# A hybrid decoder step in split fp32: grouping an item's products by the part of its weight tile

## The chip, the cores and the metric

One core of a Trainium2 chip (trn2) runs the whole step as one program. The metric is the device time of one execution in microseconds (us). The profile is one further execution, recorded by the hardware profiler.

## The reference

One layer of a hybrid decoder, for 512 prompt tokens and 8 x 4 sample tokens, all in fp32, with D = 2048:

```
h   = rms_norm(x, norm_mix_w)
b_a, c_a, h_a, q, k, v, z, a, b = split(h @ w_in)            # 7 x 1024 + 16 columns
y_a = rms_norm(b_a * dwconv3(c_a * h_a))                     # 8 channel groups
o   = rms_norm(gated_delta(silu(dwconv4(q, k, v)), a, b)) * silu(z)   # 8 heads of 128
x  += concat(y_a, o) @ w_out                                 # 2048 x 2048
h   = rms_norm(x, norm_ffn_w)
x  += square(relu(h @ w_up)) @ w_down                        # 2048 x 8192 and back
return rms_norm(x, final_norm_w), new conv states, new delta states
```

Nearly all of the arithmetic is in the four matrix products (w_in, w_out, w_up, w_down). The delta rule is a chain of small triangular systems and state updates for each head.

## The kernel before

**Split products.** TensorE multiplies fp32r values, which hold fewer bits than fp32. So each operand is split into a rounded part (hi) and the remainder (lo = value - hi), and a product is the sum of three matmuls: w_hi with x_hi, w_hi with x_lo, w_lo with x_hi. All three add up in one PSUM tile. A matmul takes a 128x128 block of a weight and 272 columns (256 prompt and 16 sample tokens) of the activations; the two halves of the tokens are h = 0 and 1.

**The stream of weights.** Weights come in items of up to 128x1024, eight blocks. `weight` (L110) loads an item by SyncE's DMA queue into a raw tile (w_raw, 2 buffers), ScalarE converts it to w_hi (L118), VectorE subtracts to w_lo (L121); both have 3 buffers. `ahead` (L46) asks for an item two items before it is multiplied. In the order of instructions, an item of eight blocks and one half is 24 matmuls, one with both halves 48.

**Where the products are issued.** `product` (L139) issues the three matmuls of one block (six with both halves), then the next block follows. It is called in the first stage (L248: three slabs of w_in against k tiles as x arrives; each item has blocks of two k tiles), in the rest of w_in (L855), in the output projection in two parts (w_o1, L906, and w_o2, L942), in the plain up blocks (L975), in w_d0 (L1178) and in the last part of w_down (L1266). From there on, up and down are done by a bilinear scheme (`bilinear`, L1064) with seven products in place of eight for a 2x2 block of weights and activations, in the order 1, 2, 5, 6, 7, 3, 4; it has a copy of the three-matmul loop (L1088). Its weights are sums of four quarters (w_q): VectorE forms w_s (L1052) and the other sums (L1054 to L1056) from loaded quarters, then ScalarE converts (L1060) and VectorE subtracts (L1061). The results are copied to u by ScalarE (L1121) or added (L1127 up, L897 down) by VectorE.

**Side work.** During w_in, the delta rule of four groups of heads runs between the projection's matmuls. `run_side` (L802) lets a generator issue its next part after every 12 matmuls of the projection. One group's chain is: an elimination loop on VectorE (L556, L560), a way through DRAM into tn and tt, a transpose of tn (L574), triangular products on TensorE (L594, L606, L611, L617, L623) with copies by VectorE between them, then four steps along the sequence (L637 to L663: st times k, r times tt, y times ke). The sum of squares of x (ssq, L246) feeds the first norm (`rstd_rows`, L152).

**What sets the order.** A scheduler of the tile framework orders each engine's instructions by priorities and by its own model of when operands are ready; `urgent` raises the priority of loads, conversions and of what frees PSUM. So the order on ScalarE, VectorE and SyncE's queue follows also from the order in which the code issues the products.

Of the kernel before, what the change touches and what calls it, by code (L numbers as in the profile page):

```python
# [18 lines left out]
P = 128  # L19
D = 2048  # L20
KT = D // P
# [11 lines left out]
N_START = 3  # L33
# [3 lines left out]
N1 = 8  # L37
# [18 lines left out]
def trunk(ctx, tc, a):  # L56
    nc = tc.nc
    V, S, G, PE = nc.vector, nc.scalar, nc.gpsimd, nc.tensor
# [77 lines left out]
            V.scalar_tensor_tensor(lo, src, w, hi.bitcast(F32), MUL, SUB)  # L136
        return hi, lo

    def product(ps, w, c, x, start, stop, halves=(0, 1)):  # L139

        (whi, wlo), (xhi, xlo) = w, x
        for i, (wp, xp) in enumerate(((whi, xhi), (whi, xlo), (wlo, xhi))):
            for h in halves:
                x = xp[h] if isinstance(xp, tuple) else xp[:, h, :]
                PE.matmul(ps[h], wp[:, c : c + P], x, start=start and i == 0, stop=stop and i == 2)  # L145

    def rstd_rows(out, ssqs, t, halves=(0, 1)):

# [29 lines left out]
    with ExitStack() as mix:  # L178
# [39 lines left out]
        for kp in range(KT // 2):  # L218
            with urgent():
                xr = tile_in(dp, "xr", [P, 2, 2, HT], tag=("gt", "qd", "vs")[kp % 3])  # L220

            def first():
                h_x.append(split(xr[:, 0], 0))

            with urgent():
                if kp:
                    nc.sync.dma_start(xr, a["x"][kp])
                else:
                    nc.sync.dma_start(nv, a["nv"])
                    tc.keep_in_program_order(nc.sync.dma_start(xr[:, 0], a["x"][kp][:, 0]))  # L230
            w = weight(a["w_first"][kp], 2 * N_START * P, None if kp else first)
            if kp == 0:
                with urgent():
                    tc.keep_in_program_order(nc.sync.dma_start(xr[:, 1], a["x"][kp][:, 1]))
            for j in range(2):
                k = 2 * kp + j
                with urgent():
                    if k:
                        h_x.append(split(xr[:, j], k))
                    sq = tmp2()  # L240
                    square = S.activation(sq, xr[:, j], AF.Square)
                    if k == 0:
                        tc.keep_in_program_order(square)
                        V.tensor_copy(ssq, sq)
                    else:
                        (G if k < KT - 2 else V).tensor_tensor(ssq, ssq, sq, ADD)  # L246
                for s in range(N_START):
                    product(first_ps[s][0], w, (j * N_START + s) * P, h_x[k], k == 0, k == KT - 1)  # L248
            if kp == 3:
                with urgent():  # L250
                    nc.sync.dma_start(wab, a["w_ab"])
# [597 lines left out]
        for (s, hf), w in ahead(srcs, lambda it: weight(a["w_in"][2 * it[0] + it[1]], 1024)):  # L849
            if hf == 0:  # L850
                job = next(jobs)
                ps = ps_big()
            for k in range(8):
                kk = 8 * hf + k
                product(ps[0], w, k * P, h_x[kk], kk == 0, kk == KT - 1)  # L855
                if k % 2:
                    run_side()
            if hf == 1:
                job(ps)
        assert next(jobs, None) is None  # L860
# [39 lines left out]
    for (ob, q), w in ahead([(o, q) for o in range(KT) for q in range(2)],  # L900
                            lambda it: weight(a["w_o1"][2 * it[0] + it[1]], N1 // 2 * P)):
        if q == 0:
            ps = ([ps_small(HT) for _ in range(2)], None) if ob in (2, 3) else ps_big()
        for k in range(N1 // 2):
            kk = N1 // 2 * q + k
            product(ps[0], w, k * P, cat[kk], kk == 0, kk == N1 - 1)  # L906
        if q == 1 and ps[1] is not None:
            add(x2[ob], ps[1])
        elif q == 1:
            for h in range(2):  # L910
                add(x2[ob][:, h], ps[0][h])
# [26 lines left out]
    steps = [(h, o) for h in range(2) for o in range(KT)]  # L938
    for (h, ob), w in ahead(steps, lambda it: weight(a["w_o2"][it[1]], N2 * P)):
        ps = ps_small(HT)  # L940
        for k in range(N2):
            product({h: ps}, w, k * P, cat[N1 + k], k == 0, k == N2 - 1, (h,))  # L942
        add(x2[ob][:, h], ps)
        sq = tile_in(sqp, "sq", [P, HT])
        S.activation(sq, x2[ob][:, h], AF.Square)
        if ob == 0:
            G.tensor_copy(ssq[:, h, :], sq)
        else:
            (G if ob < KT - 2 else V).tensor_tensor(ssq[:, h, :], ssq[:, h, :], sq, ADD)
        if ob % 2:  # L950
            nc.gpsimd.dma_start(x2_d[ob // 2][:, :, h, :], x2p[ob // 2][:, :, h, :])
        if h == 1:
            if ob == 1:
                rstd_rows(r2, [ssq], t_tile("rt", "T")[:, 0:2], (0,))
            if ob >= 2 and ob % 2 == 0 or ob == KT - 1:
                i = ob // 2 - 1 if ob < KT - 1 else KT // 2 - 1
                normalise(i, 0)
                hi, lo = c_tile(hlp, "c0_hi"), c_tile(hlp, "c0_lo")
                parts_into(hi, lo, x2p[i][:, :, 0, :])
                h_c[i].update({1: (hi[:, 0], lo[:, 0]), 2: (hi[:, 1], lo[:, 1])})  # L960
# [4 lines left out]
    def plain(m, h):  # L965
        t = t_tile("u", "u")
        u = t[:, :2]
        for i in range(2):
            ps = ps_small(HT)
            for j in range(2):  # L970
                with urgent():
                    w = weight(a["w_up"][m, 2 * i + j], 1024)
                for k in range(KT // 2):
                    x = h_c[k][1 + j] if h == 0 else (d_c[k][0][:, j], d_c[k][1][:, j])
                    product({h: ps}, w, k * P, tuple((t, t) for t in x), j == k == 0, j == 1 and k == 7, (h,))  # L975
            with urgent():
                S.activation(u[:, i], ps, AF.Relu)
        with urgent():
# [85 lines left out]
    def bilinear(items, early, cs, outs):  # L1064
# [13 lines left out]
        for (w, p), (whi, wlo) in ahead(items, load):  # L1078
# [3 lines left out]
                w.ps["y" if p == 2 else "z"] = bank(False)  # L1082
            ps = w.ps[{2: "y", 5: "z", 3: "z"}.get(p, "x")]
            c = cs(w.key)
            for k, ck in enumerate(c):
                xhi, xlo = ck[p]
                for j, (wp, xp) in enumerate(((whi, xhi), (whi, xlo), (wlo, xhi))):
                    PE.matmul(  # L1088
                        ps, wp[:, k * P : (k + 1) * P], xp,
                        start=p in (1, 2, 5) and k == j == 0, stop=k == len(c) - 1 and j == 2,  # L1090
                        skip_group_check=True,
                    )
            w.out(p, ps)

    T_AT = {1: 0, 3: 1, 2: 2, 6: 3, 5: 4, 7: 5, 4: 6}
# [77 lines left out]
    for q, w in ahead(range(KT // 4), lambda q: weight(a["w_d0"][q], 1024)):  # L1173
        for j in range(4):
            ob = 4 * q + j
            ps = [bank(True), bank(False)]
            for k in range(2):
                product(ps, w, (2 * j + k) * P, u_0[k], k == 0, k == 1)  # L1178
            for h in range(2):
                add(x2[ob][:, h], ps[h])  # L1180
    late.close()
# [78 lines left out]
    for (h, q), ws in ahead(steps, lambda it: last_weight(it[1]), 1):  # L1260
        for j in range(2):
            ob = 2 * q + j
            x = x2[ob][:, h]
            ps = ps_small(HT)
            for k in range(4):
                product({h: ps}, ws[j], k * P, u[k], k == 0, k == 3, (h,))  # L1266
            add(x, ps)
            sq = tile_in(cmb2, "sq", [P, 2, HT], tag="c")
            with urgent():
# [148 lines left out]
```

## Time and profile before

| | us |
|---|---|
| median of 3 runs (lowest, highest) | 2495.59 (2492.95, 2500.96) |
| the profiled execution | 2508.89 |
| span of its trace | 2507.1 |
| TensorE busy in it | 2435.8 |
| VectorE, ScalarE, GpSimdE busy | 1821.1, 1105.4, 498.3 |
| mean granted TensorE clock | 0.979 |

The stages in the trace, by the time at which their matmuls run: first stage 0 to 53, w_in with the delta groups 53 to 860, w_o1 860 to 955, w_o2 955 to 1052, plain up 1052 to 1133, bilinear up 1133 to 1762, w_d0 1762 to 1796, bilinear down 1796 to 2434, the last part of down 2437 to 2492, the final norm to the end. In the trace's rows an engine's idle time stands in brackets with what ended it. "PEld" is TensorE's weight load, which overlaps matmuls. A matmul's recorded duration (290 ns) is longer than the distance from one start to the next (about 125 ns), since matmuls are pipelined.

### The profile page before, as it was taken

To read this page: it belongs to the slowest core of one execution; us is meant where nothing else is said; L and a number is where in the kernel's file an instruction comes from. 1 tells how busy PE (TensorE), PEld (TensorE's weight loads), DVE (VectorE), ACT (ScalarE), POOL (GpSimd) and SP (SyncE) were. 2 spreads that over 40 slices of the span, in tenths; PEclk is the share of its full clock that TensorE was granted. 3 is DMA by queue.
4 is the path that set the end of the run, shared out by engine and by line. 5 is a ranking of instruction groups with operands and counts; after the bars stand their busy time and mean duration, and the time that the engine had idled before them with its cause. 6 is when DMAs were issued, how large, how long until landed. Compare 5 with 4: busy or idle time off the path is not lost.

```text
span 2507.1 us, 47369 instructions
## 1 busy us (share of the span) xinstructions
PE 2435.8 (97%) x19065; PEld 2389.9 (95%) x19065; DVE 1821.1 (73%) x2993; ACT 1105.4 (44%) x1628; POOL 498.3 (20%) x783
## 2 busy tenths in 40 slices
PE   8999999999999999999999999999899999999997
PEld 8999999999999899989999999999799999999996
DVE  8676575567557635788888888888488787878795
ACT  5425333332532524565555555555233333333346
POOL 4124113212312303310111111111401111111003
PEclk9999998999998999999999999999899999999998
DMA  6233333332423536565565555556846666566323
GB/s 197 91 106 110 94 101 98 112 97 88 135 88 92 200 106 205 187 195 200 193 228 195 195 194 189 188 190 220 320 127 195 195 195 193 191 194 193 108 84 106
DMA packets 145812, 400.76 MB, mean 160 GB/s; under 512 B 35540, under 2 KB 46456, under 8 KB 145592
## 3 DMA queue, kind: packets, MB, share of 16 engines
q1 hardware_dynamic: 109368, 265.56, 33.7%
q0 software_dynamic: 36224, 132.16, 14.6%
q8 instruction: 150, 2.46, 0.4%
q14 instruction: 70, 0.57, 0.1%
HBM read 318.76 MB, written 78.89 MB: 159 GB/s over the span
## 4 chain that ended last, share of the span: by engine, by line
PE 56%; issue 23%; DVE 9%; DMA 6%; POOL 3%; ACT 2%; SPq 0%; POOLq 0%; DVEq 0%; ACTq 0%
PE ps_big L145 25%; PE ps_s L1088 23%; PE ps_sm L145 3%; DVE w_lo L121 3%; DMA w_raw<-in_w_o_dram 2%; DMA w_raw<-in_w_up_dram 1%; POOL ucd L1106 1%; POOL ucd L1105 1%; DMA w_q<-in_w_d_dram 1%; ACT w_hi L118 1%; DVE xm L560 1%; PE ps_s L145 1%; DVE tm L556 1%; DMA tn<-ti 1%; DVE x2v L897 1%
## 5 line engine op out<-in xcount | busy, mean ns | idle before, releaser
L1088 PE MATMUL ps_s<-uc,w_hi 128*128 128x272 f32 x3248 | 621.1, 291 | 10.8 <-ACT w_hi L1060 8.3
L1060 ACT ACTIVATE w_hi<-w_q 128x768 fp32r<-128x768 f32 (+6 forms) x440 | 382.6, 873 | 544.7 <-PE ps_s L1088 395.3
L1088 PEld LDWEIGHTS ps_s<-uc,w_hi 128*128 128x128 f32 x3248 | 510.8, 189 | 20.4 <-ACT w_hi L1060 11.4
L1061 DVE TENSOR_TENSOR w_lo<-w_q,w_hi 128x768 fp32r<-128x768 f32 (+6 forms) x440 | 434.2, 989 | 61.0 <-ACT w_hi L1060 58.3
L1088 PE MATMUL ps_s<-uc,w_lo 128*128 128x272 f32 x1624 | 462.9, 289 | 0.3
L145 PE MATMUL ps_big<-x_hi,w_hi 128*128 128x272 f32 x1984 | 425.1, 294 | 0.9 <-ACT x_hi L133 0.7
L145 PE MATMUL ps_big<-x_hi,w_lo 128*128 128x272 f32 x1984 | 420.8, 292 | 2.4 <-DVE w_lo L121 2.4
L145 PE MATMUL ps_big<-x_lo,w_hi 128*128 128x272 f32 x1984 | 420.5, 293 | 0.3 <-DVE x_lo L136 0.3
L118 ACT ACTIVATE w_hi<-w_raw 128x1024 fp32r<-128x1024 f32 (+3 forms) x211 | 206.9, 980 | 402.9 <-PE ps_big L145 249.5
L121 DVE TENSOR_TENSOR w_lo<-w_raw,w_hi 128x1024 fp32r<-128x1024 f32 (+3 forms) x211 | 269.8, 1279 | 138.5 <-ACT w_hi L118 135.8
L145 PEld LDWEIGHTS ps_big<-x_hi,w_hi 128*128 128x128 f32 x1984 | 317.2, 190 | 5.0 <-issue 1.4
L145 PEld LDWEIGHTS ps_big<-x_hi,w_lo 128*128 128x128 f32 x1984 | 316.3, 191 | 3.9 <-DVE w_lo L121 3.0
L145 PEld LDWEIGHTS ps_big<-x_lo,w_hi 128*128 128x128 f32 x1984 | 315.9, 191 | 0.9 <-DVE x_lo L136 0.5
L1088 PEld LDWEIGHTS ps_s<-uc,w_lo 128*128 128x128 f32 x1624 | 304.6, 189 | 2.3 <-DVE w_lo L1061 1.9
L1088 PE MATMUL ps_s<-c_hi,w_lo 128*128 128x272 f32 x928 | 267.7, 289 | 2.2 <-DVE w_lo L1061 1.5
L1088 PE MATMUL ps_s<-c_hi,w_hi 128*128 128x272 f32 x928 | 266.6, 287 | 0.5 <-ACT w_hi L118 0.5
L1088 PE MATMUL ps_s<-c_lo,w_hi 128*128 128x272 f32 x928 | 266.3, 287 | 0.0
L1159 POOL DMA_DIRECT2D uc<-ucd x203 | 110.4, 548 | 439.5 <-PE ps_s L1088 411.0
L897 DVE TENSOR_TENSOR x2v<-x2v,ps_s 128x272 f32<-128x272 f32 x347 | 148.6, 434 | 67.5 <-PE ps_s L1088 59.1
L1088 PEld LDWEIGHTS ps_s<-c_hi,w_lo 128*128 128x128 f32 x928 | 174.4, 188 | 3.2 <-DVE w_lo L1061 2.1
L1088 PEld LDWEIGHTS ps_s<-c_hi,w_hi 128*128 128x128 f32 x928 | 174.5, 188 | 0.7 <-ACT w_hi L118 0.7
L1088 PEld LDWEIGHTS ps_s<-c_lo,w_hi 128*128 128x128 f32 x928 | 174.5, 188 | 0.0
(378 smaller groups left out, 4270.7 us busy)
## 6 DMA issues: line engine op xcount, KB each, us to landing
w_q<-in_w_up_dram SPq DMA_DIRECT2D x116, 512.0 KB, 4.3
uc<-ucd POOLq DMA_DIRECT2D x203, 272.0 KB, 5.3
w_raw<-in_w_in_dram SPq DMA_DIRECT2D x106, 512.0 KB, 3.4
w_q<-in_w_d_dram SPq DMA_DIRECT2D x128, 384.0 KB, 3.7
w_raw<-in_w_o_dram SPq DMA_DIRECT2D x32, 512.0 KB, 3.4
ucd<-u_hi POOLq DMA_DIRECT2D x29, 544.0 KB, 5.4
ucd<-tc POOLq DMA_DIRECT2D x29, 544.0 KB, 6.7
w_raw<-in_w_up_dram SPq DMA_DIRECT2D x28, 512.0 KB, 3.6
```

The costliest lines, as they stand in the source:

```text
L118: S.activation(hi[:, c], raw[:, c], AF.Copy)
L121: V.tensor_tensor(lo[:, c], raw[:, c], hi[:, c].bitcast(F32), SUB)
L145: PE.matmul(ps[h], wp[:, c : c + P], x, start=start and i == 0, stop=stop and i == 2)
L556: V.tensor_tensor(t, xm[:, :, j : j + 1].broadcast_to([P, 8, n]), um[:, j : j + 1, j + 1 :].broadcast_to([P, 8, n]), MUL,)
L560: V.tensor_tensor(xm[:, :, j + 1 :], xm[:, :, j + 1 :], t, SUB)
L897: V.tensor_tensor(out, out, ps, ADD)
L1060: S.activation(hi, s, AF.Copy)
L1061: V.tensor_tensor(lo, s, hi.bitcast(F32), SUB)
L1088: PE.matmul(ps, wp[:, k * P : (k + 1) * P], xp, start=p in (1, 2, 5) and k == j == 0, stop=k == len(c) - 1 and j == 2, skip_group_check=True,)
L1105: nc.gpsimd.dma_start(d[:, at : at + n], hi.bitcast(F32))
L1106: nc.gpsimd.dma_start(d[:, 7 + at : 7 + at + n], src)
L1159: nc.gpsimd.dma_start(t.bitcast(F32), uc_d[KS[j]][:, 2 * b : 2 * b + 2])
```

## The change

Within an item, the matmuls are ordered by the part of the weight. For all its blocks come w_hi with x_hi and w_hi with x_lo, block by block, and then for all its blocks w_lo with x_hi. In the first stage, whose items hold blocks of two k tiles, the passes are w_hi with x_hi, w_lo with x_hi, w_hi with x_lo, each over all blocks of the item. `products` is a generator that yields after every six (block, pass) pairs where side work runs between them, which is again every 12 matmuls. The matmuls are the same, as are the numbers of all other instructions. `start` and `stop` go to the first and the last matmul on a PSUM tile. The core of the diff:

```diff
-    def product(ps, w, c, x, start, stop, halves=(0, 1)):
-        (whi, wlo), (xhi, xlo) = w, x
-        for i, (wp, xp) in enumerate(((whi, xhi), (whi, xlo), (wlo, xhi))):
-            for h in halves:
-                x = xp[h] if isinstance(xp, tuple) else xp[:, h, :]
-                PE.matmul(ps[h], wp[:, c : c + P], x, start=start and i == 0, stop=stop and i == 2)
+    def products(w, items, start, stop, halves=(0, 1), every=0, passes=((0, 0), (0, 1), (1, 0))):
+        if passes[1][0] == 0:
+            order = [(it, i) for it in items for i in range(2)] + [(it, 2) for it in items]
+        else:
+            order = [(it, i) for i in range(3) for it in items]
+        ends = {id(ps[h]): n for n, ((ps, c, x), i) in enumerate(order) for h in halves}
+        begun = set()
+        for n, ((ps, c, x), i) in enumerate(order):
+            wp, xp = w[passes[i][0]], x[passes[i][1]]
+            for h in halves:
+                key = id(ps[h])
+                PE.matmul(ps[h], wp[:, c : c + P], xp[h] if isinstance(xp, tuple) else xp[:, h, :],
+                          start=start and key not in begun, stop=stop and ends[key] == n)
+                begun.add(key)
+            if every and n % every == every - 1:
+                yield
...
-                for s in range(N_START):
-                    product(first_ps[s][0], w, (j * N_START + s) * P, h_x[k], k == 0, k == KT - 1)
+            items = [(first_ps[s][0], (j * N_START + s) * P, h_x[2 * kp + j]) for j in range(2) for s in range(N_START)]
+            product(w, items, kp == 0, kp == KT // 2 - 1, passes=((0, 0), (1, 0), (0, 1)))
...
-            for k in range(8):
-                kk = 8 * hf + k
-                product(ps[0], w, k * P, h_x[kk], kk == 0, kk == KT - 1)
-                if k % 2:
-                    run_side()
+            for _ in products(w, [(ps[0], k * P, h_x[8 * hf + k]) for k in range(8)], hf == 0, hf == 1, every=6):
+                run_side()
...
-            for k, ck in enumerate(c):
-                xhi, xlo = ck[p]
-                for j, (wp, xp) in enumerate(((whi, xhi), (whi, xlo), (wlo, xhi))):
-                    PE.matmul(
-                        ps, wp[:, k * P : (k + 1) * P], xp,
-                        start=p in (1, 2, 5) and k == j == 0, stop=k == len(c) - 1 and j == 2,
-                        skip_group_check=True,
-                    )
+            seq = [(k, whi, i) for k in range(len(c)) for i in range(2)] + [(k, wlo, 0) for k in range(len(c))]
+            for n, (k, wp, i) in enumerate(seq):
+                PE.matmul(
+                    ps, wp[:, k * P : (k + 1) * P], c[k][p][i],
+                    start=p in (1, 2, 5) and n == 0, stop=n == len(seq) - 1, skip_group_check=True,
+                )
```

`product` is now a call of `products` that runs it to its end; the other calls (w_o1, w_o2, plain up, w_d0, the last part of down) pass all blocks of an item at once. In the changed file, line numbers after `product` are higher by 7 to 15.

The scheduler's order follows. First TensorE in the first delta group, where r = vs is multiplied by tt (L643 before, L658 after) and y, copied from that result, by ke (L651, then L666); `ps_big` rows are the projection's (L145, then L152). Before:

```order
690 L145 MATMUL ps_big<-x_hi,w_lo 128x272
691 L643 MATMUL ps_sm<-vs,tt 128x128 x2
692 L145 MATMUL ps_big<-x_hi,w_lo 128x272
693 L145 MATMUL ps_big<-x_hi,w_hi 128x272 x2
694 L145 MATMUL ps_big<-x_lo,w_hi 128x272 x2
695 L145 MATMUL ps_big<-x_hi,w_lo 128x272 x2
696 L145 MATMUL ps_big<-x_hi,w_hi 128x272 x2
697 L145 MATMUL ps_big<-x_lo,w_hi 128x272 x2
698 L145 MATMUL ps_big<-x_hi,w_lo 128x272 x2
699 L145 MATMUL ps_big<-x_hi,w_hi 128x272
700 L651 MATMUL ps_sm<-y,ke 128x128
```

And after, at the same place:

```order
517 L152 MATMUL ps_big<-x_hi,w_lo 128x272 x7
518 L658 MATMUL ps_sm<-vs,tt 128x128 x2
519 L152 MATMUL ps_big<-x_hi,w_lo 128x272
520 L152 MATMUL ps_big<-x_hi,w_hi 128x272
521 L666 MATMUL ps_sm<-y,ke 128x128
522 L152 MATMUL ps_big<-x_hi,w_hi 128x272
523 L666 MATMUL ps_sm<-y,ke 128x128
524 L677 MATMUL ps_sm<-at,y 128x128 x2
```

Fourteen matmuls of the projection stood between the two steps, and two stand there now. The w_lo matmuls of several blocks stand together (x7).

Second, VectorE in the middle of the bilinear down stage: w_s (L1052, then L1061) is the sum of two newly loaded quarters, `x2v` rows are the additions of a product to the residual (L897, then L909), `w_lo` rows the subtractions (L1061, then L1070). Before:

```order
2038 L897 TENSOR_TENSOR x2v_20191<-x2v_20191,ps_s 128x272
2039 L1061 TENSOR_TENSOR w_lo<-w_q,w_hi 128x768
2040 L897 TENSOR_TENSOR x2v_20191<-x2v_20191,ps_s 128x272
2041 L1052 TENSOR_TENSOR w_s_22203<-w_q 128x768
2042 L1061 TENSOR_TENSOR w_lo<-w_q,w_hi 128x768
```

After:

```order
1992 L909 TENSOR_TENSOR x2v_20191<-x2v_20191,ps_s 128x272
1993 L1070 TENSOR_TENSOR w_lo<-w_q,w_hi 128x768
1994 L1061 TENSOR_TENSOR w_s_22203<-w_q 128x768
1995 L909 TENSOR_TENSOR x2v_20191<-x2v_20191,ps_s 128x272
1996 L1070 TENSOR_TENSOR w_lo<-w_q,w_hi 128x768
```

The sum w_s stood behind the addition and stands ahead of it now.

More of the change, by code (lines that the diff above doesn't have):

```diff
@@ L137, in split, with product @@
         return hi, lo
-    def product(ps, w, c, x, start, stop, halves=(0, 1)):
-        (whi, wlo), (xhi, xlo) = w, x
-        for i, (wp, xp) in enumerate(((whi, xhi), (whi, xlo), (wlo, xhi))):
-            for h in halves:
-                x = xp[h] if isinstance(xp, tuple) else xp[:, h, :]
-                PE.matmul(ps[h], wp[:, c : c + P], x, start=start and i == 0, stop=stop and i == 2)
+    def products(w, items, start, stop, halves=(0, 1), every=0, passes=((0, 0), (0, 1), (1, 0))):
[7 more added lines that the diff above has]
+            wp, xp = w[passes[i][0]], x[passes[i][1]]
+            for h in halves:
+                key = id(ps[h])
[4 more added lines that the diff above has]
+                yield
+    def product(*args, **kw):
+        for _ in products(*args, **kw):
+            pass
     def rstd_rows(out, ssqs, t, halves=(0, 1)):
@@ L903, in trunk @@
             ps = ([ps_small(HT) for _ in range(2)], None) if ob in (2, 3) else ps_big()
-        for k in range(N1 // 2):
-            kk = N1 // 2 * q + k
-            product(ps[0], w, k * P, cat[kk], kk == 0, kk == N1 - 1)
+        product(w, [(ps[0], k * P, cat[N1 // 2 * q + k]) for k in range(N1 // 2)], q == 0, q == 1)
         if q == 1 and ps[1] is not None:
@@ L940, in trunk @@
         ps = ps_small(HT)
-        for k in range(N2):
-            product({h: ps}, w, k * P, cat[N1 + k], k == 0, k == N2 - 1, (h,))
+        product(w, [({h: ps}, k * P, cat[N1 + k]) for k in range(N2)], True, True, (h,))
         add(x2[ob][:, h], ps)
@@ L972, in plain @@
                     w = weight(a["w_up"][m, 2 * i + j], 1024)
-                for k in range(KT // 2):
-                    x = h_c[k][1 + j] if h == 0 else (d_c[k][0][:, j], d_c[k][1][:, j])
-                    product({h: ps}, w, k * P, tuple((t, t) for t in x), j == k == 0, j == 1 and k == 7, (h,))
+                xs = [h_c[k][1 + j] if h == 0 else (d_c[k][0][:, j], d_c[k][1][:, j]) for k in range(KT // 2)]
+                items = [({h: ps}, k * P, tuple((t, t) for t in x)) for k, x in enumerate(xs)]
+                product(w, items, j == 0, j == 1, (h,))
             with urgent():
@@ L1176, in trunk @@
             ps = [bank(True), bank(False)]
-            for k in range(2):
-                product(ps, w, (2 * j + k) * P, u_0[k], k == 0, k == 1)
+            product(w, [(ps, (2 * j + k) * P, u_0[k]) for k in range(2)], True, True)
             for h in range(2):
@@ L1264, in trunk @@
             ps = ps_small(HT)
-            for k in range(4):
-                product({h: ps}, ws[j], k * P, u[k], k == 0, k == 3, (h,))
+            product(ws[j], [({h: ps}, k * P, u[k]) for k in range(4)], True, True, (h,))
             add(x, ps)
```

## The prediction

> **What bounds the kernel now.** I read the page first, then the busy time by stage, the waits of TensorE, and the stretches around its longest waits. The page's span and its engine row say who is full:
>
> ```profile
> span 2507.1 us, 47369 instructions
> PE 2435.8 (97%) x19065; PEld 2389.9 (95%) x19065; DVE 1821.1 (73%) x2993; ACT 1105.4 (44%) x1628; POOL 498.3 (20%) x783
> PEclk9999998999998999999999999999899999999998
> ```
>
> TensorE is busy for 97% of the span, and there is one weight load for each matmul, so no load is saved now where two matmuls in a row use one weight block. Stage by stage (first projection with its side work, second half of the output projection and the plain up blocks, bilinear up, the step over to down, bilinear down; columns as in the page, then clock, DMA share, GB/s):
>
> ```profile
> 53.00:860.00 807.00, 798.64 (x6407) 783.83 (x6407) 527.40 (x1188) 305.72 (x548) 215.66 (x344) 0.97 0.33 104
> 960.00:1160.00 200.00, 188.15 (x1445) 182.43 (x1444) 147.21 (x219) 108.37 (x162) 55.94 (x58) 1.00 0.62 205
> 1160.00:1745.00 585.00, 582.26 (x4587) 576.37 (x4587) 483.46 (x554) 340.03 (x413) 61.35 (x113) 1.00 0.56 195
> 1745.00:1830.00 85.00, 70.09 (x473) 66.38 (x472) 47.37 (x107) 21.39 (x38) 34.83 (x64) 0.90 0.83 302
> 1830.00:2400.00 570.00, 568.70 (x4476) 562.32 (x4475) 459.57 (x666) 214.52 (x262) 79.84 (x147) 1.00 0.55 174
> ```
>
> The two long bilinear stretches leave 2.7 of 585 and 1.3 of 570 us idle: over 1,155 us a new order has nothing to win. A matmul there takes 585/4587 = 0.127 us, whichever weight part it reads. Idle time lies at 960 to 1160 (11.9 us) and 1745 to 1830 (14.9 us); the first projection loses 8.4 us, and more by its clock of 0.97. TensorE's waits (engine, line, what it waited for: us, times, longest):
>
> ```profile
> PE ps_s L1088 <- ACT w_hi L1060: 8.3, 6, 3.1
> PE ps_sm L145 <- DVE w_lo L121: 6.9, 12, 2.0
> PE ps_s L1088 <- DVE w_lo L1061: 6.4, 7, 2.1
> PE ps_s L145 <- DVE x2v L897: 6.3, 2, 6.1
> PE ps_sm L594 <- DVE tn L574: 4.5, 4, 1.9
> PE ps_sm L152 <- DVE ssq L246: 3.0, 1, 3.0
> PE ps_big L145 <- DVE w_lo L121: 2.4, 3, 1.1
> PE ps_s L1088 <- DVE w_lo L121: 0.7, 1, 0.7
> ```
>
> The rows for w_lo, which the change bears on, add up to 6.9 + 6.4 + 2.4 + 0.7 = 16.4 us, 0.65% of the span. That is the ceiling for the waits themselves.
>
> **What the change does to the need for w_lo.** An item of 24 matmuls takes 24 x 0.127 = 3.0 us. Before, its third matmul reads w_lo; after, the seventeenth does: 14 x 0.127 = 1.78 us of slack more. w_hi is needed at the same moment as before. Its last use comes 7 matmuls earlier (16th instead of 23rd, 0.9 us), so ACT can refill that slot sooner; w_lo's slot is released at the item's end as before. The counts of matmuls, conversions and DMAs stay the same. The clearest case in the trace, TensorE then VectorE:
>
> ```profile
> 1281.17 0.29 PE L1088 MATMUL ps_s<-d_hi,w_hi 128*128 128x272 f32 x1
> 1281.30 0.28 PE L1088 MATMUL ps_s<-d_lo,w_hi 128*128 128x272 f32 x1
> 1283.66 0.39 PE L1088 MATMUL ps_s<-d_hi,w_lo 128*128 128x272 f32 x1 [2.08 <-DVE w_lo L1061]
> ```
>
> ```profile
> 1281.24 1.23 DVE L1052 TENSOR_TENSOR w_s<-w_q 128x1024 f32<-128x1024 f32 x1 [1.38 <-DMA w_q<-in_w_up_dram]
> 1282.39 1.22 DVE L1061 TENSOR_TENSOR w_lo<-w_q,w_hi 128x1024 fp32r<-128x1024 f32 x1
> ```
>
> Two matmuls of the item run, then TensorE stands for 2.08 us: w_lo's subtraction was queued on VectorE behind a sum that waited for a transfer. After the change 14 more matmuls fill 1.78 us of that.
>
> **The clock.** A wait costs more than its length where it halves the clock. The stretches around the two longest waits for w_lo, and those of the four delta groups:
>
> ```profile
> 1154.90:1158.30 3.40, 1.42 (x11) 1.20 (x10) 3.40 (x5) 1.34 (x2) 0.00 (x0) 1.00 0.54 178
> 1158.30:1161.70 3.40, 3.40 (x17) 3.40 (x16) 2.64 (x3) 0.00 (x0) 0.00 (x0) 0.50 0.77 213
> 1281.20:1284.60 3.40, 1.32 (x11) 1.11 (x10) 3.35 (x3) 1.93 (x3) 0.55 (x1) 1.00 1.01 391
> 1284.60:1288.00 3.40, 3.40 (x17) 3.40 (x16) 2.77 (x6) 0.19 (x1) 0.00 (x0) 0.50 1.02 384
> ```
>
> ```profile
> 180.00:200.00 20.00, 20.00 (x167) 18.50 (x164) 10.80 (x30) 2.20 (x5) 4.29 (x6) 0.57 0.13 41
> 385.00:410.00 25.00, 23.15 (x181) 21.42 (x182) 12.41 (x35) 3.27 (x7) 5.23 (x7) 0.59 0.18 48
> 593.00:612.00 19.00, 16.83 (x194) 14.86 (x192) 13.06 (x42) 3.40 (x8) 5.45 (x7) 1.00 0.22 63
> 793.00:817.00 24.00, 22.59 (x186) 20.60 (x185) 13.31 (x38) 3.28 (x7) 5.81 (x7) 0.64 0.12 35
> ```
>
> After a stretch of 3.4 us with only 1.3 to 1.4 us of matmuls, the next 3.4 us ran at half clock and lost 1.7 us. In the delta groups the clock stayed down far longer: 20 x 0.43 = 8.6, 25 x 0.41 = 10.2 and 24 x 0.36 = 8.6 us were lost in groups one, two and four, nothing in group three.
>
> **What the change costs.** The order of the changed kernel has the first matmul of the delta chain (L594, which reads tn) after 1,182 matmuls of the projection instead of 1,188, and likewise six earlier in the other groups. What it waits for does not get earlier:
>
> ```profile
> 178.25 0.41 PE L145 MATMUL ps_big<-x_hi,w_lo 128*128 128x272 f32 x2
> 178.50 0.42 PE L145 MATMUL ps_big<-x_hi,w_hi 128*128 128x272 f32 x2
> 179.80 0.37 PE L594 MATMUL ps_sm<-tn,at 32*32 32x32 f32 x6 [0.88 <-DVE tn L574]
> ```
>
> ```profile
> 179.30 0.45 DVE L574 STREAM_TRANSPOSE tn<-tn 128x256 f32<-128x256 f32 x1 [0.79 <-DMA tn<-ti]
> ```
>
> The transpose waits for a transfer behind VectorE's elimination loop, and the order has the same VectorE instructions in that stretch as before. So TensorE arrives 6 x 0.125 = 0.75 us sooner (pairs start 0.25 us apart above) and waits that much longer.
>
> **The sum**, on the profiled execution (2508.89 us, of which 2507.1 are span):
> - First stage: the three waits of 2.4 us in all end ahead of the 3.0-us wait for ssq, whose chain they do not feed: that one takes up what they release. 0 (bounds -2.4 and +1: the last lows come later in each pair of k tiles).
> - 960 to 1160: VectorE is full where the waits lie (3.40 of 3.40 us at 1154.90), so w_lo comes no sooner, and 1.78 us of slack is won once for the cluster, not at each wait: -1.8. Bounds 0 and, if each of its waits went by itself, 16.4 - 2.4 - 2.1 = -11.9. I take the low end because VectorE's row is full.
> - The halving at 1158 goes with it: -1.7 (or 0, if 1.3 us of the wait remain in one stretch).
> - 1281: -1.8, and its halving -1.7.
> - Delta groups: 4 x 0.75 = +3.0 (bounds 0, if later waits in the chain shrink alike, and +3.0). The step from L643 to L651 has 2 matmuls to cover the copy of y where it had 14: I put +0.2 on each group, +0.8 (bounds 0 and 4 x 0.88, the tn wait being the nearest hand-over of a small tile).
> - Group three stands at the edge: its stretch escaped with a wait like those of one and four, and with 0.75 us more it would probably halve. That costs 8.6, less some 1.5 us of its waits that slower matmuls would fill: 7.1. I put half in the sum, +3.5.
> - The step over to down (6.3 for x2v, 8.3 for w_hi) hangs on transfers; w_hi is needed as early as before. 0 +- 1.7, one halving.
>
> Sum: -1.8 - 1.7 - 1.8 - 1.7 + 3.0 + 0.8 + 3.5 = +0.3 us, on 2508.9. The median of the runs shown is 2495.59, 13.3 below the profiled one; carried over as a difference, 2495.9. I say 2495.5.
>
> [...]
>
> **Rivals.** A measurement of this kernel tells about 0.3%, 7.5 us, from no change.
> - *The waits for w_lo go, and the delta groups cost nothing.* Then it is -7.0 alone (2488.6), and with every wait of the 16.4 gone and the two halvings, -19.8: 2475.8. For it: the slack of 1.78 us exceeds every wait but a few of about 2. Against it: VectorE and the transfers are the supply there and get no faster. Faster by over 0.3% needs over half a microsecond beyond the -7.0. Chance 0.27.
> - *The delta groups halve more often (slower).* The unprofiled runs lie 13.3 us lower, which two groups fewer at half clock would explain (2 x 7.1). If the longer wait for tn then halves all four each time, two more groups cost 14.2, and with 3.8 and -7.0 the kernel is at +11.0: 2506.6. It decides from two more halved groups on. [...] Against it: that the profiled run halves more than others is not shown. Chance 0.20.
> - *VectorE's waits move in front of TensorE (slower).* In the bilinear down stage the sum w_s, which waits for its transfer, now stands one add earlier in VectorE's queue, and that add and the next w_lo stand behind it:
>
> ```profile
> DVE w_s L1052 <- DMA w_q<-in_w_d_dram: 29.9, 36, 3.3
> ```
>
>   TensorE feels none of these 29.9 us now (1.3 us idle in that stage). If a third came through, +10 on +0.3: 2505.8. w_lo being wanted 14 matmuls later speaks against it. Chance 0.03.
> - *Repeated weights make matmuls faster.* The change of block from one matmul to the next happens as often as before (high of k, then another block), and loads equal matmuls on the page: no gain. Under 0.01.
>
> **Numbers.** Forecast, no change that can be told, around 2495.5: 0.50. Its own range is 2488 to 2503. The rest, 0.27 and 0.23, lies on either side; to leave out no more than 2 in 10 the range runs from 2483 (between -7.0 and -19.8) to 2508 (the second rival with a little over its price).
>
> **What would show it.** Right: the w_lo rows of L145 and L1088 after 960 us fall from about 14 to under 8 us; 1158 and 1284 run at full clock; L594's row rises from 4.5 to about 7.5; the two bilinear stretches stay within 2 us. The prediction is wrong if the w_lo waits vanish without other waits in their place (faster), if the clock at 593 to 612 and the others falls to 0.6 with more lost than 27 us in the four groups (slower), or if new waits on u or x2v appear at every block of the bilinear stages.

## The result, and the profile after

The changed kernel takes 2564.72 us (median of 4 runs, 2553.47 to 2573.97) against 2498.28 us of the kernel before on the same chip: a ratio of 1.0262, 95% interval 1.0233 to 1.0291. It is slower by 2.6%, some 66 us; I had forecast no change and put the end of the range at 2508.

The page of the changed kernel, its span and engines:

```profile
span 2567.8 us, 47386 instructions
PE 2450.4 (95%) x19065; PEld 2402.2 (94%) x19065; DVE 1791.7 (70%) x2993; ACT 1098.7 (43%) x1628; POOL 487.2 (19%) x783
```

The counts of instructions on the five engines are those of before, and VectorE is busy for less time (1791.7 us, it was 1821.1): there is no more work. TensorE's busy time for the same 19065 matmuls has grown by 14.6 us (2435.8 before); most of the rest is waiting. Where: in both kernels the last matmul on a ps_big tile (the first projection and most of w_o1) starts at 952 us (951.9 before, 952.6 after) and the bilinear up stage at 1133 (1133.7, 1133.1). From there, the busy time by stage, bilinear up and then down, from first to last matmul. Before:

```profile
1133.70:1759.70 626.00, 617.91 (x4850) 610.34 (x4849) 514.40 (x594) 357.99 (x440) 69.90 (x129) 0.99 0.57 200
1796.30:2437.10 640.80, 629.70 (x4876) 618.15 (x4875) 516.09 (x810) 239.79 (x319) 92.84 (x171) 0.99 0.55 174
```

After:

```profile
1133.10:1798.50 665.40, 631.70 (x4849) 621.69 (x4849) 510.36 (x594) 352.86 (x444) 70.51 (x130) 0.98 0.54 189
1835.40:2497.00 661.60, 631.29 (x4878) 618.97 (x4877) 504.97 (x810) 239.58 (x320) 92.52 (x169) 0.99 0.55 167
```

Up takes 39.4 us more and down 20.8: 60.2 of the 60.7 us by which the span grew. These are the two stages in which I had seen nothing to win. In down nearly all of it is idle time of TensorE. In up 25.6 us are, and the other 13.8 us are in its busy time (617.91 to 631.70 us for the same matmuls), at a mean granted clock of 0.98 where it was 0.99: a third of the loss there shows as slower matmuls. TensorE's longest waits now:

```profile
PE ps_s L1096 <- ACT u L1128: 29.6, 33, 4.4
PE ps_s L1096 <- DVE x2v L909: 20.6, 32, 1.7
PE ps_s L1096 <- ACT w_hi L1069: 11.7, 11, 3.8
PE ps_sm L152 <- ACT w_hi L118: 11.0, 9, 4.1
PE ps_sm L609 <- DVE tn L589: 5.4, 4, 1.6
PE ps_big L152 <- DVE w_lo L121: 1.8, 2, 0.9
```

The waits for w_lo are gone but for 1.8 us, as the change means them to be. In their place TensorE waits for PSUM banks: in up for the copy of a result to u (29.6 us), in down for the addition to the residual (20.6). VectorE makes the addition itself; the copy is ScalarE's, whose queue waits for VectorE, as the rows further down show. VectorE's own waits say why both are late:

```profile
DVE w_s L1061 <- DMA w_q<-in_w_up_dram: 68.6, 26, 4.2
DVE w_s L1061 <- DMA w_q<-in_w_d_dram: 66.8, 39, 9.6
```

The sum w_s waits 68.6 us for the loads of up, and 66.8 us for those of down (29.9 before). In the kernel before, its row over the stretch of up, 1133 to 1760 us, was

```profile
DVE w_s L1052 <- DMA w_q<-in_w_up_dram: 1.5, 2, 1.4
```

One turn of the loop in up, VectorE's queue first (idle time and its releaser in brackets), then SyncE's four loads of quarters, then ScalarE, then TensorE:

```profile
1400.39 1.01 DVE L935 TENSOR_TENSOR u<-u,u_hi 128x816 fp32r<-128x816 f32 x1
1401.32 0.43 DVE L1134 TENSOR_TENSOR u<-u,ps_s 128x272 f32<-128x272 f32 x1
1401.67 1.22 DVE L1070 TENSOR_TENSOR w_lo<-w_q,w_hi 128x1024 fp32r<-128x1024 f32 x1
1402.80 1.28 DVE L935 TENSOR_TENSOR tc<-tc,u_hi 128x1088 fp32r<-128x1088 f32 x1
1404.01 2.35 DVE L1070 TENSOR_TENSOR w_lo<-w_q,w_hi 128x1024 fp32r<-128x1024 f32 x2
1409.96 0.44 DVE L1134 TENSOR_TENSOR u<-u,ps_s 128x272 f32<-128x272 f32 x1 [3.61 <-PE ps_s L1096]
1410.32 1.22 DVE L1070 TENSOR_TENSOR w_lo<-w_q,w_hi 128x1024 fp32r<-128x1024 f32 x1
1413.83 1.23 DVE L1061 TENSOR_TENSOR w_s<-w_q 128x1024 f32<-128x1024 f32 x1 [2.29 <-DMA w_q<-in_w_up_dram]
1414.97 0.43 DVE L1134 TENSOR_TENSOR u<-u,ps_s 128x272 f32<-128x272 f32 x1
1415.32 1.22 DVE L1070 TENSOR_TENSOR w_lo<-w_q,w_hi 128x1024 fp32r<-128x1024 f32 x1
1416.45 1.22 DVE L1064 TENSOR_TENSOR w_q<-w_s,w_q 128x1024 f32<-128x1024 f32 x1
```

```profile
1399.33 7.38 SPq L1051 DMA_DIRECT2D w_q<-in_w_up_dram  x4
```

```profile
1401.49 1.11 ACT L934 ACTIVATE u_hi<-tc 128x1088 fp32r<-128x1088 f32 x1 [2.95 <-DVE u L935]
1402.50 1.04 ACT L1069 ACTIVATE w_hi<-w_q 128x1024 fp32r<-128x1024 f32 x1
1403.45 0.38 ACT L1128 ACTIVATE u<-ps_s 128x272 f32<-128x272 f32 x1
```

```profile
1403.88 0.39 PE L1096 MATMUL ps_s<-d_hi,w_hi 128*128 128x272 f32 x1 [1.61 <-ACT u L1128]
```

The copy of u that frees TensorE's bank (L1128, 1403.45) stands on ScalarE behind a conversion that waited 2.95 us for VectorE (L935, 1400.39), and VectorE came to that late: it had stood for 4.2 us before the w_s of this turn (until 1390.57) and worked without a gap since. The last of the four loads goes out at about 1406.4, when the two w_lo subtractions that read the old quarters end (1404.01 + 2.35). It takes 7 us; until 1413.83 VectorE stands before w_s. Behind w_s are queued an addition to u, the next w_lo, and all the work up to the next pair of w_lo subtractions, which alone lets the next load go. So, by these rows, a late load makes the next load late. How often w_s comes round can be read from its first and last start in a stretch. Before, in the middle of up:

```profile
L1052 DVE TENSOR_TENSOR w_s<-w_q x17: 1217/1217/1217, 1379.5 to 1719.2; 128x1024 f32<-128x1024 f32 x17
```

After:

```profile
L1061 DVE TENSOR_TENSOR w_s<-w_q x15: 1224/1226/1229, 1390.6 to 1708.7; 128x1024 f32<-128x1024 f32 x15
```

(1719.2 - 1379.5)/16 = 21.23 us a pair before, with no wait for a load; (1708.7 - 1390.6)/14 = 22.72 after. For 28 pairs 1.49 us more each are 41.7 us, about the whole loss of up (39.4). TensorE was busy in up for 617.91 us with 4872 matmuls, which is 21.3 us for a pair's 168, as long as the round: before, TensorE set the pace. How much shorter the loop of VectorE and the loads was then, this period doesn't say.

In down, VectorE then TensorE:

```profile
2123.84 0.96 DVE L1061 TENSOR_TENSOR w_s<-w_q 128x768 f32<-128x768 f32 x1 [1.57 <-DMA w_q<-in_w_d_dram]
2124.71 0.43 DVE L909 TENSOR_TENSOR x2v<-x2v,ps_s 128x272 f32<-128x272 f32 x1
```

```profile
2122.28 0.91 PE L1096 MATMUL ps_s<-uc,w_lo 128*128 128x272 f32 x6
2123.03 1.41 PE L1096 MATMUL ps_s<-uc,w_hi 128*128 128x272 f32 x10
2125.20 1.77 PE L1096 MATMUL ps_s<-uc,w_hi 128*128 128x272 f32 x12 [0.77 <-DVE x2v L909]
```

The addition that frees a bank stands behind w_s, and the next matmul waits for it. The last matmuls of its product end at 2123.19 in the rows (2122.28 + 0.91), and VectorE, idle until 2123.84, does w_s first: the addition starts at 2124.71, when w_s is all but over (2123.84 + 0.96).

### The profile page after: what moved, and what is told of

Read it like the earlier page. It is cut to its first block, busy times and chain, and to the rows that moved or that the text cites. A ratio compares the mean times of both kernels' runs of the same rounds, so it can differ in the third digit from the quotient of the medians.

```text
span 2567.8 us, 47386 instructions
## 1 busy us (share of the span) xinstructions
PE 2450.4 (95%) x19065; PEld 2402.2 (94%) x19065; DVE 1791.7 (70%) x2993; ACT 1098.7 (43%) x1628; POOL 487.2 (19%) x783
## 4 chain that ended last, share of the span: by engine, by line
PE 34%; DMA 11%; DVE 9%; issue 8%; ACT 4%; POOL 0%; SPq 0%; DVEq 0%; ACTq 0%; POOLq 0%
PE ps_s L1096 29%; DMA w_q<-in_w_d_dram 5%; PE ps_big L152 3%; DVE w_lo L1070 2%; DMA w_q<-in_w_up_dram 2%; DMA w_raw<-in_w_o_dram 2%; PE ps_sm L152 2%; DMA w_raw<-in_w_up_dram 2%; DVE x2v L909 1%; DVE w_lo L121 1%; ACT w_hi L1069 1%; ACT w_hi L118 1%; DVE x2v L1246 0%; DMA w_raw<-in_w_d_dram 0%; PE ps_s L152 0%
## 5 line engine op out<-in xcount | busy, mean ns | idle before, releaser
L1096 PE MATMUL ps_s<-uc,w_hi 128*128 128x272 f32 x3248 | 472.9, 291 | 30.2 <-DVE x2v L909 20.6
L1096 PEld LDWEIGHTS ps_s<-uc,w_hi 128*128 128x128 f32 x3248 | 431.3, 189 | 42.1 <-DVE x2v L909 27.8
L1070 DVE TENSOR_TENSOR w_lo<-w_q,w_hi 128x768 fp32r<-128x768 f32 (+6 forms) x440 | 430.6, 985 | 2.9 <-ACT w_hi L1069 2.4
L152 PE MATMUL ps_big<-x_hi,w_hi 128*128 128x272 f32 x1984 | 420.1, 293 | 2.7 <-ACT x_hi L129 1.7
L152 PE MATMUL ps_big<-x_lo,w_hi 128*128 128x272 f32 x1984 | 418.5, 292 | 0.0
L152 PEld LDWEIGHTS ps_big<-x_hi,w_hi 128*128 128x128 f32 x1984 | 316.7, 191 | 6.2 <-ACT x_hi L129 1.9
L152 PEld LDWEIGHTS ps_big<-x_lo,w_hi 128*128 128x128 f32 x1984 | 313.9, 190 | 0.5 <-DVE x_lo L130 0.2
L152 PE MATMUL ps_big<-x_hi,w_lo 128*128 128x272 f32 x1984 | 287.6, 293 | 1.8 <-DVE w_lo L121 1.8
L152 PEld LDWEIGHTS ps_big<-x_hi,w_lo 128*128 128x128 f32 x1984 | 266.0, 191 | 3.9 <-DVE w_lo L121 2.2
L1096 PE MATMUL ps_s<-uc,w_lo 128*128 128x272 f32 x1624 | 256.3, 289 | 0.1
L1096 PE MATMUL ps_s<-c_hi,w_hi 128*128 128x272 f32 x928 | 238.1, 289 | 3.7 <-ACT w_hi L1069 2.4
L1096 PE MATMUL ps_s<-c_lo,w_hi 128*128 128x272 f32 x928 | 238.0, 289 | 0.0
L1096 PEld LDWEIGHTS ps_s<-uc,w_lo 128*128 128x128 f32 x1624 | 225.1, 190 | 0.5 <-DVE w_lo L1070 0.5
L909 DVE TENSOR_TENSOR x2v<-x2v,ps_s 128x272 f32<-128x272 f32 x347 | 148.5, 433 | 103.0 <-PE ps_s L1096 96.5
L1061 DVE TENSOR_TENSOR w_s<-w_q 128x768 f32<-128x768 f32 (+4 forms) x74 | 73.5, 994 | 135.3 <-DMA w_q<-in_w_up_dram 68.6
L1096 PE MATMUL ps_s<-d_hi,w_hi 128*128 128x272 f32 x464 | 132.1, 311 | 29.7 <-ACT u L1128 29.6
```

Of the source, the lines that this page charges most:

```text
L152: PE.matmul(ps[h], wp[:, c : c + P], xp[h] if isinstance(xp, tuple) else xp[:, h, :], start=start and key not in begun, stop=stop and ends ...
L909: V.tensor_tensor(out, out, ps, ADD)
L1061: V.tensor_tensor(self.s1, a21, a22, ADD)
L1070: V.tensor_tensor(lo, s, hi.bitcast(F32), SUB)
L1096: PE.matmul(ps, wp[:, k * P : (k + 1) * P], c[k][p][i], start=p in (1, 2, 5) and n == 0, stop=n == len(seq) - 1, skip_group_check=True,)
```

## The experiments

Theory A: the scheduler moved w_s forward in VectorE's queue; there it waits for a load, and the loop through VectorE and the loads becomes longer than TensorE's part. Theory B: the loss is TensorE's and ScalarE's new order, above all that in up only 4 matmuls of product 3, and no longer 11, are taken ahead to keep TensorE busy while u is copied, and that ScalarE converts the sums ahead of that copy.

### The bilinear loop back in its old order

```diff
-            seq = [(k, whi, i) for k in range(len(c)) for i in range(2)] + [(k, wlo, 0) for k in range(len(c))]
-            for n, (k, wp, i) in enumerate(seq):
+            for k, ck in enumerate(c):
+                xhi, xlo = ck[p]
+                for j, (wp, xp) in enumerate(((whi, xhi), (whi, xlo), (wlo, xhi))):
...
```

> The change with its bilinear loop put back to the order of before (each block's three matmuls together), and grouped in all other stages. All theories of the loss place it in the two bilinear stages, whose matmuls took 629.0 and 640.8 us before and 668.3 and 661.6 us after: the time should fall by about 60 us, to 2491 to 2502 us (before: 2498.3). What is left against before is the worth of the grouping elsewhere: by the trace of the changed kernel +0.7 us up to 952 us and -1.3 us from there to the bilinear stage. If the time stays above 2530 us, the loss is not in the order of the bilinear matmuls.

(The stage lengths named there, 629.0 and 668.3, run to the last matmul of up. The rows above end 3 us earlier in both kernels, where its last product begins: 626.0 and 665.4.)

Measured: 2506.09 us, ratio to before 1.0019 (1.0000 to 1.0037). The loss is in the bilinear loop, all of it. The grouping in all the other stages brings nothing: it costs 0 to 0.4%.

### The changed kernel with w_s queued where it stood

```diff
+    def behind(x, y):
+        if x is not None and y is not None:
+            tc.add_manual_dep(x.ins, y.ins.name, mybir.DependencyInfo(
+                mybir.DependencyClass.NoSync, mybir.DependencyReason.DATA), reason="order")
...
-                    V.tensor_tensor(self.s1, a21, a22, ADD)
+                    self.at['s'] = V.tensor_tensor(self.s1, a21, a22, ADD)
+                    behind(self.at['s'], self.prev and self.prev.at.get(2 if n == 1024 else ('o', 6)))
```

This run is called pin below. `self.prev` is the pair before, `at` holds its w_lo subtractions by product and, under 'o', its additions. The edge orders the queue and adds no wait.

> The changed kernel, all stages grouped, with one edge of order on VectorE: the sum w_s of a pair of quarters is queued behind the subtraction of w_lo for product 2 of the pair before (up) or behind the addition after product 6 of the pair before (down), about where it stood before the change. TensorE's order keeps its 4 hoisted matmuls of product 3 (11 before). Theory A (w_s waits at the head of VectorE's queue for a transfer, what stands behind it releases the buffers of the next transfers, and the loop is longer than TensorE's 21 us): most of the 60 us come back, 2495 to 2515 us, the waits of w_s fall from 135 us in all to under 45. Theory B (the loss comes from TensorE's own order, 4 matmuls in place of 11 to cover the copy of u, and from ScalarE's order): no more than 15 us come back, 2550 us or more, and the waits for u stay near 30 us.

Measured: 2501.52 us, ratio 1.0010 (0.9996 to 1.0023): all 63 us come back with one instruction put back. VectorE's waits before w_s in this run, and its round in up:

```profile
DVE w_s L1068 <- DMA w_q<-in_w_d_dram: 13.0, 9, 3.6
DVE w_s L1068 <- DMA uc<-ucd: 10.9, 1, 10.9
DVE w_s L1068 <- DMA w_q<-in_w_up_dram: 7.6, 8, 1.8
```

```profile
L1068 DVE TENSOR_TENSOR w_s<-w_q x17: 1217/1225/1226, 1375.2 to 1715.5; 128x1024 f32<-128x1024 f32 x17
```

The waits for quarters fall from 135.4 to 20.6 us, and the round is (1715.5 - 1375.2)/16 = 21.27 us. In up TensorE's order is still that of the changed kernel, with 4 matmuls taken ahead: counted in the two traces, 28 of up's 4872 bilinear matmuls stand elsewhere. So in up, where the time falls from 665.4 to 626.0 us, theory B is out. In down the edge changed TensorE's queue too, since the scheduler fills all queues anew (306 of 4872 places; 10 matmuls of a later product were taken ahead, now 5): there w_s and the order of the matmuls moved together, and this run doesn't tell them apart.

### The kernel before with w_s moved forward

```diff
...
+                    if self.prev and n == 1024:
+                        behind(self.prev.at.get(2), self.at['s'])
+                        behind(self.prev.at['a11'], self.at['s'])
+                    elif self.prev:
+                        behind(self.prev.at.get(('o', 6)), self.at['s'])
```

> The kernel before, its matmuls in the old order, with edges of order on VectorE only: in up the sum w_s stands ahead of the w_lo subtraction for product 2 and the sum a11 of the pair before it, in down ahead of the addition after product 6, as in the changed kernel. Theory A: it gets slower though no matmul has moved, 2520 to 2560 us, with waits of w_s for its transfer of 1.5 us or more per pair in up and new waits of TensorE for u and x2v. Theory B: TensorE's and ScalarE's orders are those of before, so 2490 to 2505 us.

Measured: 2584.49 us, ratio 1.0324 (1.0307 to 1.0341). It is slower than the changed kernel, though the code issues the matmuls in the old order. In up TensorE's queue is that of before (24 of 4872 places differ); in down the scheduler changed it (714 of 4872 places), so up alone is a clean trial. By stage, up then down, and w_s's waits:

```profile
1130.10:1790.30 660.20, 623.36 (x4850) 612.20 (x4849) 513.04 (x594) 358.80 (x441) 69.41 (x129) 0.99 0.55 189
1826.60:2512.80 686.20, 642.44 (x4876) 619.97 (x4874) 515.91 (x810) 237.15 (x320) 92.77 (x172) 0.99 0.51 162
```

```profile
DVE w_s L1059 <- DMA w_q<-in_w_d_dram: 68.8, 40, 8.4
DVE w_s L1059 <- DMA w_q<-in_w_up_dram: 50.5, 25, 6.0
```

Theory A's sign and stages hold; the size was beyond my range: up loses 34.2 us, down 45.4. TensorE's waits name the places: in down 36.3 us for x2v, in up 32.4 us for w_lo, which in the old matmul order is wanted early. For u, which I had expected, it waits 1.4 us in up. So w_s at the head of the queue harms through whatever TensorE wants next behind it. Down loses more here than in the changed kernel (45.4 against 20.8); whether the grouping helps there is not shown, since the matmuls of down were reordered.

### The sum formed by GpSimd

```diff
-                    V.tensor_tensor(self.s1, a21, a22, ADD)
+                    G.tensor_tensor(self.s1, a21, a22, ADD)
```

> The changed kernel with the sum w_s formed by GpSimd instead of VectorE, so that VectorE's queue no longer waits for that transfer; the order of ScalarE's and TensorE's rows in the bilinear loop stays that of the changed kernel (4 hoisted matmuls, the conversion of the sums ahead of the copy of u). Theory A (the wait at the head of VectorE's queue): the waits go to GpSimd, and 30 to 60 us come back, 2500 to 2535 us; what stays would be the slower sum there and VectorE slowed beside it. Theory B (orders on TensorE and ScalarE): stays within 10 us of the changed kernel's 2564.7 us.

Measured: 2511.8 us, ratio 1.0052 (1.0031 to 1.0073): 53 of 66 us come back. GpSimd now waits before w_s, the two rows of its waits, while up takes 639.5 us and down 643.9:

```profile
POOL w_s L1061 <- DMA w_q<-in_w_up_dram: 226.9, 28, 13.1
POOL w_s L1061 <- DMA w_q<-in_w_d_dram: 167.8, 34, 13.8
```

```profile
1137.40:1776.90 639.50, 619.51 (x4850) 611.83 (x4849) 481.43 (x565) 358.25 (x444) 141.15 (x157) 0.99 0.56 197
1807.30:2451.20 643.90, 631.09 (x4878) 619.54 (x4878) 479.57 (x766) 239.47 (x320) 178.14 (x217) 0.99 0.56 175
```

The wait for the load is 395 us on GpSimd and does little harm, since little stands behind it on that engine. VectorE still waits for this sum, at the subtraction (L1063) that overwrites a quarter which the sum reads:

```profile
DVE w_q L1063 <- POOL w_s L1061: 156.8, 66, 7.1
```

That is more than the 135.4 us which it waited for the loads in the changed kernel. But in up this subtraction stands behind the addition to u, the sum a11 and the w_lo for product 2, the three that had come to stand behind w_s. So, by these rows, not the length of the wait decides but what is queued behind it. One thing stays mixed in: VectorE is also relieved of the sum itself (481.43 us busy in up, 510.36 in the changed kernel). Its 565 other instructions there take 481.43 us where they took 474.9 (510.36 less 35.5 for the 29 sums, 1.23 us each), and GpSimd is busy for 141.15 us where it was 70.51, some 2.4 us more for each sum. TensorE's order in up is again that of the changed kernel (20 of 4872 places differ; in down 334), and its waits there for the copy of u are 15.0 us where they were 29.6 us.

### How much has to move

Both kernels are the changed one, with w_s in up held between two neighbours; down is left as in the change. First, only the w_lo subtraction for product 2 stands behind w_s:

```diff
+                    behind(self.at['s'], self.prev and self.prev.prev and n == 1024 and self.prev.prev.at.get(('o', 3)) or None)
+                    if self.prev and n == 1024:
+                        behind(self.prev.at.get(2), self.at['s'])
```

> The changed kernel; in up the sum w_s is queued ahead of one instruction more than where it does no harm, the w_lo subtraction for product 2 of the pair before (1.13 us of VectorE's time). Down is left as in the change. Theory A as a closed loop (work on VectorE from one w_s to the last w_lo of the pair, then the load into the quarter that it frees, then the next w_s): what is moved in front of the wait lengthens the loop one for one, once its slack against TensorE's 21 us is used. The changed kernel moves 2.6 us and loses 39.6 us in 28 pairs, 1.4 each, so the slack is about 1.2 us: with 1.13 us moved, up should take 626 to 635 us (after: 665.4, pin: 625.8), and the kernel some 20 us more than pin for its down stage, 2518 to 2530 us. Rival C (w_s only delays what happens to stand behind it, each time anew): the loss goes with the waiting instructions, and up loses about half of the 39.6, 640 to 650 us.

Then the sum a11 too:

```diff
+                        behind(self.prev.at['a11'], self.at['s'])
```

> As the run before, with the sum a11 queued behind w_s too: 2.27 us are moved. Closed loop with 1.2 us of slack: 28 x (2.27 - 1.2) = 30 us, up 650 to 660 us, the kernel 2540 to 2555 us. Rival C: no more than 5 us beyond the run before, since a11 is no nearer to TensorE than the product-2 subtraction.

Measured: 2555.77 us (ratio 1.0224, 1.0197 to 1.0251) and 2552.01 us (1.0213, 1.0188 to 1.0238). The first is 26 us beyond my range for the closed loop with slack, the second inside the range but no slower than the first. Up took 651.4 us in the first profile and 664.1 in the second: both above what I had reckoned (626 to 635, and 650 to 660), the first next to rival C's 640 to 650. w_s's rounds, first one and then the other:

```profile
L1068 DVE TENSOR_TENSOR w_s<-w_q x16: 1224/1226/1227, 1385.8 to 1715.0; 128x1024 f32<-128x1024 f32 x16
```

```profile
L1068 DVE TENSOR_TENSOR w_s<-w_q x16: 1224/1226/1226, 1374.4 to 1709.9; 128x1024 f32<-128x1024 f32 x16
```

21.95 and 22.37 us a pair, against 21.27 (pin) and 22.72 (the change). So one slack of 1.2 us doesn't describe them. By the second run and the change it would be about 1.2 (2.27 us moved cost 1.10 a pair, 2.6 cost 1.45), by the first under half a microsecond (1.13 us moved cost 0.68). In this stretch w_s waited for a load at none of its 17 turns in the kernel before, at 5 of 17 in pin, and at all 16 in these two: with the grouped order, and w_s where it stood, little was left. My down stage was wrong too: it lost 30 us in the first of these runs (666.6 against 636.8 in pin), where I reckoned 20. What stays open is how the loss grows with what is moved: the rounds rise in order, but the profile of the second kernel was its slowest execution (2574.56), and the medians don't tell the two apart. In two respects rival C did better: in its figure for up, and in that a11 added nothing to the time.

### w_in in its old order, the rest grouped and pinned

```diff
-            for _ in products(w, [(ps[0], k * P, h_x[8 * hf + k]) for k in range(8)], hf == 0, hf == 1, every=6):
-                run_side()
+            for k in range(8):
+                kk = 8 * hf + k
+                product(w, [(ps[0], k * P, h_x[kk])], kk == 0, kk == KT - 1)
+                if k % 2:
+                    run_side()
```

The first stage is put back in the same way.

> Grouped in the output projection, plain up, bilinear (with w_s queued as in the run called pin), w_d0 and the last part; the first stage and w_in in the order of before. If the delta groups pay for the grouping of w_in (my prediction: +3.0 by the earlier wait for tn, +0.8, and +3.5 for a halved clock), this is some 7 us below the run with everything grouped and pinned, 2493 to 2496 us; if they don't, within 3 us of it (2501.5).

Measured: 2501.15 us, ratio 1.0008 (0.9993 to 1.0023), 0.4 us from the run with all grouped and pinned (ratio 1.0010). The delta groups do not pay measurably for the grouping. Yet the third group's clock fell, as I had said it might: 580 to 625 us, in the changed kernel and in this one:

```profile
580.00:625.00 45.00, 42.54 (x364) 39.54 (x363) 27.72 (x73) 12.19 (x24) 14.95 (x19) 0.89 0.24 70
```

```profile
580.00:625.00 45.00, 42.98 (x398) 40.26 (x397) 30.59 (x84) 16.53 (x29) 18.11 (x25) 1.00 0.32 96
```

In all six profiles with w_in grouped that group's clock was between 0.89 and 0.92, in all five with the old order 1.00. In the other groups it came and went in both (group one at 1.00 in four of the eleven).

### Only w_o2 and plain up grouped

The kernel before, with these two calls changed as in the diff of the change:

```diff
-        for k in range(N2):
-            product({h: ps}, w, k * P, cat[N1 + k], k == 0, k == N2 - 1, (h,))
+        product(w, [({h: ps}, k * P, cat[N1 + k]) for k in range(N2)], True, True, (h,))
...
-                for k in range(KT // 2):
-                    x = h_c[k][1 + j] if h == 0 else (d_c[k][0][:, j], d_c[k][1][:, j])
-                    product({h: ps}, w, k * P, tuple((t, t) for t in x), j == k == 0, j == 1 and k == 7, (h,))
+                product(w, items, j == 0, j == 1, (h,))
```

> The kernel before with only w_o2 and the plain up blocks grouped (a few calls in other stages go block by block through the new helper, in the old order). My prediction's term for this cluster: -1.8 for the slack and -1.7 for the halving at 1158, so 2496.8 us and, in the trace, the bilinear stage starting about 2 us earlier after the end of the tiles ps_big (before: 1133.7 - 951.9 = 181.8 us). If every wait of the cluster counted by itself, up to 10 us less. If w_hi, wanted as early as ever, takes the place of w_lo: no change of more than 1 us.

Measured: 2499.39 us, ratio 1.0004 (0.9984 to 1.0024); from the last ps_big matmul to the bilinear stage 1124.2 - 942.6 = 181.6 us (181.8 before). TensorE's waits from 940 to 1140 us in this run:

```profile
PE ps_sm L152 <- ACT w_hi L118: 7.7, 8, 1.9
```

Before, the row in that place was 6.9 us for w_lo. It is 7.7 us for w_hi now: the other half of the same supply takes its place at once.

### Down alone grouped, with w_s held back

```diff
...
+            seq = [(k, wp, i) for k in range(len(c)) for wp, i in ((whi, 0), (whi, 1), (wlo, 0))]
+            if w.n < 1024:
+                seq.sort(key=lambda t: t[1] is wlo)
...
```

> The kernel before with the products grouped in the bilinear down stage alone, and there w_s queued behind the addition after product 6. In the two profiles with w_s so placed (pin, mixed) down took 636.8 us against 640.8 before; if that is the grouping's and not chance, the kernel gains 4 us: 2494 to 2498 us, ratio 0.998 to 0.999, at the edge of what can be told. If it was chance, ratio 1.000 and down at 640 to 641 us.

Measured: 2498.82 us, ratio 0.9997 (0.9980 to 1.0013), down 638.7 us. The 4 us are halfway there in the profile and can't be told in the time. No version tried here beats the kernel before.

## Why the prediction was wrong

- **The ceiling and the mechanism for w_lo: right.** The waits for it fell from 16.4 to 1.8 us. No time came of it: with w_s put back, up takes 626.0 us as before, so the -3.5 that I had put at 1281 and its halving don't show.
- **The cluster from 960 to 1160: -3.5 predicted, about 0 measured** (181.8 us before, 181.6 with only this stage grouped, 180.5 in the changed kernel). I had seen that VectorE is full there, and still let 1.78 us of slack through; w_hi came as late as w_lo, with 7.7 us of waits for 6.9.
- **The delta groups: +7.3 predicted, 0.4 us measured** against the run with w_in in its old order. The row of the first matmul that reads tn (L594, now L609) rose from 4.5 to 5.4 us, not 7.5: tn came earlier as well, and that matmul starts at 178.2 us in group one where it started at 179.8. In the third group the clock did fall, to 0.89 over 45 us, which is some 5 us where I had put 8.6 for a halving.
- **The step that failed: the sentence that over the two bilinear stretches "a new order has nothing to win", and the third rival at 0.03.** That rival named the mechanism, the engine and the addition behind w_s, which then came true in down, and was priced at +10 if a third of w_s's waits came through. I set it aside because "TensorE feels none of these 29.9 us now" and w_lo would be wanted later. Both looked at the wrong thing. What matters behind w_s in the changed kernel is not w_lo but what frees a PSUM bank: the addition, and the work that ScalarE's copy of u waits for. By the rows it is also what lets the next load go. And a stage that leaves TensorE 2.7 of 585 us idle says nothing of how near the next loop is: moving one 1.13-us subtraction behind w_s took the round from 21.27 to 21.95 us. The sign that I had named for being wrong came: new waits for u (29.6 us, 33 times) and x2v (20.6 us, 32 times).
- **Not looked at: up.** I compared VectorE's order in down alone. In up, where the trace of before shows w_s nearly without waits, the scheduler had moved three instructions (an addition, the w_lo for product 2, the sum a11) from ahead of w_s to behind it, two thirds of the loss (39.4 of 60.2 us). With w_s put back in both stages all of it goes (2501.52 us), with w_s moved in the old kernel it comes (2584.49 us).
- **The forecast's sum** of +0.3 us for all the rest was near by luck: with w_s put back the grouped kernel is at a ratio of 1.0010, but neither the gains of 7.0 us nor the costs of 7.3 that made the sum can be seen in the times.

What is shown: in up, where w_s stands in VectorE's queue decides the loss, and the wait harms through what is queued behind it. In down the loss comes and goes with the same edge of order, but TensorE's queue changed with it, and that the place of w_s alone does it is argued from the waits for x2v. Argued from the trace, too, is the closed loop through the load: its rounds and its reload point fit, but the trial of its size did not give the slack I reckoned. More buffers for the quarters, which would cut that loop, were not tried.

## What to carry to other kernels

A change of order on one engine is also a change of order on all engines whose queues a scheduler fills; before costing it, list for each queue which instructions that wait for a transfer have moved, what now stands behind them, and whether that includes something which releases a bank or a buffer. Here such a move cost 60 us in two stages in which the main engine was full: there, ask how long the next longest loop is, not only what the full engine waits for now. Where one instruction wanders, an edge of order on it alone tests the theory and mends the kernel.

## What the runs showed of the hardware

The same 512-KB load takes very different times. In up, the time from issue to landing of the quarters (min, median, max), before and then after:

```profile
DMA to landing us min/median/max: 3.1/4.2/6.9
```

```profile
DMA to landing us min/median/max: 3.2/5.9/7.8
```

The sizes are the same. The four loads of a turn go out within 7.4 us in the changed kernel (the SPq row above) and within 8.7 before, while GpSimd's queue writes the sums of u. What makes the median longer is not shown, and it is not what makes the kernel slower: in pin, which is as fast as before, the median is 5.3 us and the longest 8.0; in the kernel with a11 moved too, which is 2.1% slower, they are 4.4 and 7.7.

The clock did not follow the sum of TensorE's waits. In up of the changed kernel TensorE is idle for 33.7 us, with no wait over 4.4 us, at a mean granted clock of 0.98, and is busy 13.8 us longer with the same matmuls than before. In up of the old kernel with w_s moved forward it is idle for 36.8 us, at a clock of 0.99, and busy only 5.5 us longer. What sets the difference is not shown.
